# A chunked recurrence on 64x64 quarters of the TensorE array, in six slots a chunk with a fixed order on every engine

## The chip, the cores and the metric

The program runs on one core of a Trainium2 chip. The metric is the time of one execution on the device, in microseconds (us). The profile is one execution, recorded by the hardware profiler; its rows give starts from the beginning of the span.

## The reference

A trunk of two layers on 1024 tokens of width 1024. Layer 0 is attention (sliding window and dilated) and a gated feed-forward block; layer 1 is an RWKV-7 time mix and a second feed-forward block; a norm ends it. All is float32. The change lies in the time mix, whose core is a recurrence over the tokens with one 64x64 state for each of 16 heads:

```python
def step(state, inp):
    r_t, w_t, k_t, v_t, a_t, b_t = inp
    sa = jnp.einsum('bhvk,bhk->bhv', state, a_t)
    state = state * w_t[:, :, None, :] + sa[..., None] * b_t[:, :, None, :] + v_t[..., None] * k_t[:, :, None, :]
    return state, jnp.einsum('bhvk,bhk->bhv', state, r_t)
```

After it every head's output is normed over its 64 values, scaled (`lnx_w`, `lnx_b`), a bonus `sum(r*k*r_k) * v` is added, the result is multiplied by a gate `g`, and an output projection with `w_o` follows.

## The kernel before

The recurrence is computed in 16 chunks of 64 tokens (`NC`). Inside a chunk it is a set of 64x64 products for each head and one triangular solve; only the 64x64 state `S` goes from chunk to chunk. Heads stand in eight pairs, the even head on partitions 0 to 63 and the odd one on 64 to 127, and the pairs in two groups of four.

`rwkv_dense` (L1038) makes, in two halves of 512 tokens (`q`), what the chunks need, and stores it in DRAM: `ar` (decayed `kk` and `r`), `bm` and `km` (the transposed keys, with the masked products against `r` beside them), `nk`, `n` (the triangle that is to be inverted), `v`, the gate `gT` and the bonus factors `bon`. `solve` (L1071) inverts 32x32 triangles by 31 steps of two VectorE operations (L1085, L1086) and stores them as `u` and `ut`. Four solves are needed; the last, `solve(1, 1, ve)`, is handed on as a function (L1367) and runs within the recurrence, at chunk 1.

`Scan` (L1370) loads. `load` (L1428) brings a chunk's `ar`, `bm`, `km`, `nk`, `vb`, some 2 MB; `load2` (L1396) brings, for a pair of chunks, `u` and two small operands `ub` and `nb`. Each has two buffers, so loads run one chunk ahead. `inverse` (L1409) joins the 32x32 inverses of a pair of chunks to 64x64 ones: eight products `nb`, `ub`, four copies, eight products, four copies; `u`'s upper corner is copied first (L1419).

`rwkv_scan` (L1442) is the recurrence. In `step` (L1477), for each of the two groups:

- `o1`: `nk` times `vb`, plus `ar` times `S` (L1486 to L1492); the lower half feeds the solve, the upper half is part of the output.
- `rb`: the lower half, copied by ScalarE and VectorE (L1494, L1495) into the two diagonal blocks of a 128x128 tile whose other blocks are zero. `S`, `rb`, `sb`, `nk` and `vb` are all such block diagonals, so that one 128-row product serves two heads.
- `z`: `u` times `rb` (L1498), copied to `sb` in two halves (L1499, L1500).
- `o2`: `km` times `vb` plus `bm` times `sb` (L1502, L1504).
- The new state: for each head of the pairs VectorE adds `o2` and `S` (L1512), GpSimd multiplies by the decay `el` (L1513).
- The output `y`: the upper halves of `o1` and `o2` (L1519, L1520).

`finish` (L1524), once for two chunks: mean, centring, square, variance, the power -1/2 on GpSimd (L183), scaling by it and by `lw`, the bonus (`vn`, the values again, loaded by `load3` and multiplied by `bo`, L1538), eight transposes on TensorE, the gate (L1549) and the split into two float32r parts (`t.split`, L154) for the output projection.

The program is written with a scheduler that orders instructions on each engine by a simulated timeline; `chained` fixes the order within one accumulation alone. The recurrence's first instructions are thus placed among the dense stage's last. DMAs all go through SyncE's (SP's) queue, one after another; one that waits for a buffer holds back those behind it. PSUM is given out as p1, pz, p2 with two banks each and pq, pg with one.

Of the kernel before, what the change touches and what calls it, by code (L numbers as in the profile page):

```python
# [21 lines left out]
P = 128  # L22
T = 1024
# [1014 lines left out]
def rwkv_dense(t, hp, sv, hT, first):  # L1038
# [11 lines left out]
    d["bon"] = dp.tile([T, 16], F32, name="bon_d")  # L1050
# [20 lines left out]
    def solve(q, g, eng):  # L1071
# [9 lines left out]
        po.memset(u.rearrange("p i j -> p (i j)")[:, 0:1024:33], 1.0)  # L1081
        for s in range(31):
            i, j = s + 1, 31 - s
            w3 = sv.tile([P, 256], F32, name="sw", tag="sw")[:, :i * j].rearrange("p (i j) -> p i j", j=j)
            eng.tensor_tensor(w3, u[:, :i, s:s + 1].broadcast_to([P, i, j]), n[:, s:s + 1, s + 1:].broadcast_to([P, i, j]), MUL)  # L1085
            eng.tensor_tensor(u[:, :i, s + 1:], u[:, :i, s + 1:], w3, ADD)  # L1086
        ac.copy(n[0:64], u[0:64].rearrange("p i j -> p j i"))
# [7 lines left out]

        return store
# [15 lines left out]
    for q in range(2):  # L1112
# [251 lines left out]
        ve.tensor_copy(bs, transposed(bon)[:, :, 0:16])  # L1364
        nc.sync.dma_start(d["bon"][ts].rearrange("(b p) h -> p b h", p=P), bs)
    es.close()
    return d, scan, lambda: solve(1, 1, ve)  # L1367


class Scan:  # L1370


    def __init__(self, t, d):
# [4 lines left out]
        self.nb, self.ub, self.tb, self.u2 = (self.zeroed(lp, n, 1, 8, 64)[0] for n in ("nb", "ub", "tb", "u2"))  # L1378
        self.zs = [(self.zeroed(lp, "nk0", 1, 2, 5, 64)[0], self.zeroed(lp, "vb0", 1, 2, 8, 64)[0])]
        self.pools, self.us, self.tiles = [lp], [None, None], [None, None]  # L1380

    def zeroed(self, pool, name, n, *shape):
        r = [pool.tile([P, *shape], F32, name=f"{name}{i}") for i in range(n)]
        for x in r:
            self.t.nc.gpsimd.memset(x, 0.0)
        return r
# [5 lines left out]
    def more(self, sp):  # L1392
        self.pools.append(sp)
        self.zs.append((self.zeroed(sp, "nk1", 1, 2, 5, 64)[0], self.zeroed(sp, "vb1", 1, 2, 8, 64)[0]))

    def load2(self, g):  # L1396
        nc, d, half = self.t.nc, self.d, self.half
        u = self.pools[g % 2].tile([P, 8, 2, 64], F32, name="u", tag="u")
        q, i = divmod(2 * g, 8)
        nc.sync.dma_start(u, d["u"][q, :, :, i:i + 2])  # L1400
        self.us[g % 2] = [u[:, :, cc] for cc in range(2)]
# [7 lines left out]
    def inverse(self, g, pq):  # L1409

        pe, ac = self.t.nc.tensor, self.t.nc.scalar
        us = self.us[g % 2]
        ps = pq.tile([64, 8, 64], F32, name="pq", tag="pq")
# [26 lines left out]


def rwkv_scan(t, d, ld, sv, last):  # L1442

# [194 lines left out]
```

## Time and profile before

| what | us |
|---|---|
| three runs | 2832.75, 2835.06, 2835.6; median 2835.06 |
| the profiled execution | 2844.29 |
| its span | 2842.5 |
| first product with a state (chunk 1) | 1861.94 |
| first product of the output projection after the recurrence | 2072.56 |

The mean granted TensorE clock of the profiled execution is 0.967. In a row of grouped instructions the line stands first, then engine, operation, the output and the inputs by name (digits left out, so `o1` and `o2` are both `o`), the shapes, the count, and after a bar the busy time in us and the mean duration of one in ns; after the next bar the idle time of the engine before them and what ended it. A float32 matmul of the program stands as two records, each with a weight load (PEld). A matmul's shape is given as rows x columns of the array that it uses, then the moving operand.

### The profile page before, as it was taken

The numbers are of one execution on the slowest core, as the hardware profiler recorded it, in microseconds if no ns is written. First come the engines' busy times: TensorE is split into PE (matmuls) and PEld (weight loads), VectorE is DVE, ScalarE is ACT, GpSimd is POOL, SyncE is SP. The second block draws the span as 40 slices with busy tenths as digits, with TensorE's granted clock in tenths as the row PEclk, the third lists the DMA queues.
The fourth block names the chain that finished last, engine by engine and source line by source line (L and its number), as shares of the span: only waits on it lengthen the run. The fifth ranks groups of instructions, "written<-read, shape, count | busy, mean of one in ns | idle before, by whom it ended". The sixth has DMA issues, their size and how long they took to land. (4 is left out here: it accounts for less than half of the span.)

```text
span 2842.5 us, 38023 instructions
## 1 busy us (share of the span) xinstructions
PE 2660.4 (94%) x13302; PEld 2123.9 (75%) x13302; DVE 1781.8 (63%) x3017; ACT 1203.2 (42%) x2377; POOL 1101.3 (39%) x830
## 2 busy tenths in 40 slices
PE   8999997989999999998998899888998999999998
PEld 6777775678888877775676667777877888887776
DVE  4554564566434448789658888767666544344987
ACT  3445445334333333345644454434334433333434
POOL 1221221335343416445443533335643544331644
PEclk9999999999999999999999899789999999999999
DMA  4111112632222246452465276788753222225654
GB/s 139 45 38 53 38 53 80 209 106 89 80 84 85 74 159 226 148 177 89 157 165 161 82 219 162 202 210 211 209 174 104 98 81 83 81 71 196 212 156 159
DMA packets 301536, 367.18 MB, mean 129 GB/s; under 512 B 101000, under 2 KB 175112, under 8 KB 301344
## 3 DMA queue, kind: packets, MB, share of 16 engines
q1 hardware_dynamic: 296560, 351.08, 40.2%
q10 hardware_dynamic: 4496, 12.62, 1.1%
q8 instruction: 105, 1.72, 0.3%
q0 software_dynamic: 288, 1.05, 0.1%
q14 instruction: 87, 0.71, 0.1%
HBM read 268.98 MB, written 95.68 MB: 128 GB/s over the span
## 5 line engine op out<-in xcount | busy, mean ns | idle before, releaser
L919 PE MATMUL pd<-ws,as 128*128 128x512 f32 x1848 | 431.8, 395 | 24.0 <-DVE ws L154 23.0
L919 PEld LDWEIGHTS pd<-ws,as 128*128 128x128 f32 x1848 | 350.1, 190 | 103.7 <-DVE ws L154 28.6
L771 PE MATMUL y<-t,cw 128*128 128x512 f32 x1584 | 370.2, 389 | 0.0
L771 PEld LDWEIGHTS y<-t,cw 128*128 128x128 f32 x1584 | 297.3, 188 | 62.4
L154 DVE TENSOR_TENSOR cw<-raw,cw 128x512 fp32r<-128x512 f32 x264 | 216.4, 822 | 199.6 <-ACT cw L154 196.0
L154 ACT CAST cw<-raw 128x512 fp32r<-128x512 f32 x264 | 163.2, 621 | 245.8 <-PE z L771 103.3
L154 DVE TENSOR_TENSOR wl<-raw,wh 128x512 fp32r<-128x512 f32 (+1 forms) x146 | 146.0, 1002 | 105.4 <-ACT wh L154 105.3
L154 ACT CAST wh<-raw 128x512 fp32r<-128x512 f32 (+1 forms) x154 | 119.9, 779 | 205.8 <-PE mm L174 53.6
L780 POOL TENSOR_TENSOR c<-c 128x512 f32<-128x512 f32 x66 | 111.7, 1692 | 186.5 <-DVE c L787 135.3
L173 PE MATMUL mm<-hx,wh 128*128 128x512 f32 x384 | 163.8, 427 | 0.0
L775 ACT COPY sn<-y 128x512 f32<-128x512 f32 x132 | 76.9, 587 | 196.4 <-PE y L771 193.1
L175 PE MATMUL mm<-hx,wl 128*128 128x512 f32 x384 | 152.3, 397 | 0.0
L174 PE MATMUL mm<-hx,wh 128*128 128x512 f32 x384 | 151.6, 395 | 0.0
L771 PE MATMUL z<-b,cw 128*128 128x512 f32 x576 | 142.5, 398 | 6.6 <-DVE tx L717 6.6
L257 POOL TENSOR_TENSOR ry<-ry,S 128x512 f32<-128x512 f32 x40 | 51.8, 1294 | 217.2 <-DVE ry L256 192.7
L771 PEld LDWEIGHTS z<-b,cw 128*128 128x128 f32 x576 | 110.9, 193 | 31.0 <-issue 7.0
L154 ACT CAST as<-raw 128x512 fp32r<-128x512 f32 x110 | 68.2, 620 | 154.0 <-PE pd L919 81.5
L771 PE MATMUL y<-b,cw 128*128 128x512 f32 x528 | 129.0, 394 | 0.0
L771 PE MATMUL z<-t,cw 128*128 128x512 f32 x528 | 123.3, 389 | 0.0
L813 POOL TENSOR_TENSOR raw<-s,raw 128x512 f32<-128x512 f32 x44 | 59.6, 1355 | 151.8 <-DVE cw L154 151.6
L787 DVE TENSOR_TENSOR c<-z,sn 128x512 f32<-128x512 f32 x92 | 63.4, 689 | 84.8 <-ACT sn L775 74.4
L771 PE MATMUL x<-b,cw 128*128 128x512 f32 x480 | 116.1, 396 | 0.0
(469 smaller groups left out, 6129.6 us busy)
## 6 DMA issues: line engine op xcount, KB each, us to landing
raw<-act SPq DMA_DIRECT2D x132, 256.0 KB, 3.4
raw<-in_wd SPq DMA_DIRECT2D x132, 256.0 KB, 3.1
raw<-in_wg SPq DMA_DIRECT2D x88, 256.0 KB, 2.9
raw<-in_wu SPq DMA_DIRECT2D x88, 256.0 KB, 2.6
act<-c SPq DMA_DIRECT2D x88, 256.0 KB, 2.0
raw<-in_wrk SPq DMA_DIRECT2D x32, 512.0 KB, 4.4
raw<-in_win SPq DMA_DIRECT2D x24, 512.0 KB, 3.5
raw<-in_wout SPq DMA_DIRECT2D x32, 256.0 KB, 3.5
```

Source lines behind the costliest of these rows:

```text
L154: return self.nc.scalar.copy(hi, src), (eng or self.nc.vector).tensor_tensor(lo, src, hi.bitcast(F32), SUB)
L173: seen(mm(ps, lh, rh, start=start, stop=False))
L174: seen(mm(ps, lh, rl, start=False, stop=False))
L175: seen(mm(ps, ll, rh, start=False, stop=stop))
L257: nc.gpsimd.tensor_tensor(y, y, self.S[:, s], MUL)
L771: seen(pe.matmul(ps, w[:, x, s], bs[:, k, y], start=start and k == j == 0, stop=k == 3 and j == 2, skip_group_check=True))
L775: ac.copy(s, ps)
L780: po.tensor_tensor(g, g, u, MUL)
L787: ve.tensor_tensor(c[-1], z, s, ADD)
L813: po.tensor_tensor(a11, s, a11, SUB)
L919: pe(ps[b], s[:, x, t], w[:, y], start=first and i == 0, stop=f == N - 1 and i == 2, skip_group_check=True)
```

## The change

Six things change, all in the recurrence.

1. **Quarters.** No tile is a block diagonal any more. Every matmul is 64x64x64, of one head, in one quarter of the array: rows by the operands' partitions (`r`), columns by the output's (`r` or `o`, the other half). Loops go over `both`, so that the half alternates from one matmul to the next; where `to` (the new state) and `y` (the output) are made, their matmuls alternate too. The state is added to `to` by a product with an identity `eye`, and the output's `ar` part goes straight into `y`'s bank.
2. **Copies.** `rb` is one ScalarE copy of 128x256, `sb` one VectorE copy, the new state one VectorE product with the decay, `y` one ScalarE copy. GpSimd has no part in the state.
3. **Slots and order.** A chunk has six slots. Each of the two groups is a generator of three stages a chunk (up to the `rb` copy, up to the `sb` copy, up to `y`); group 0 goes in slots 0, 2 and 4, group 1 in slots 3, 5 and 1 of the next chunk. `own` chains every compute instruction of the recurrence to the one before on its engine, in written order. DMAs are not chained.
4. **Inverse, centring and finish** are cut into pieces and put in given slots. The bonus is no longer made of `vn`: `diag` makes diagonal 64x64 blocks of `bo`, and `turned` computes `v` times that block and adds the transposed `y` by products with `eye`, so that the bonus comes with the transposes.
5. **The last solve** is a generator, `solving`; it takes one step in slot 0 (its loads) and two steps a slot from slot 8 on. Its stores follow the last step.
6. **Loads** run two chunks ahead, in three buffers (`vb` in eight, since `turned` reads it later); the order of a chunk's loads is `ar`, `nk`, `vb`, `km`, `bm`. `u` keeps two buffers; `load2` of the next pair stands in slot 11 of a pair, after the middle stage of group 1 in the odd chunk. `bon` is stored with even and odd heads apart; zeroed tiles other than the inverse's four fall away.

The core of the diff:

```diff
+            xz = p1.tile([P, 2, 4, 64], F32, name="xz", tag="xz")
+            for i, e, r, o in both:
+                mm(xz[r, 0, i], nk[r, k0 + i], vb[r, k0 + i], start=i == 0, stop=c == 0)
+            if c:
+                for i, e, r, o in both:
+                    mm(xz[r, 0, i], ar[r, k0 + i, 0:64], S[r, i], start=False, stop=True)
+            rb, sb = (tp.tile([P, 4, 64], F32, name=n, tag=f"{n}{g}", bufs=1) for n in ("rb", "sb"))
+            own(ac.copy(rb, xz[:, 0]))
+            yield
+            to, y = (p2.tile([P, 4, 64], F32, name=n, tag=n) for n in ("to", "yo"))
+            if c:
+                for i, e, r, o in both:
+                    mm(to[r, i], eye[r], S[r, i], start=i == 0, stop=False)
+                    mm(y[o, i], ar[r, k0 + i, 64:], S[r, i], start=i == 0, stop=False)
+            for i, e, r, o in both:
+                mm(to[r, i], km[r, k0 + i, 0:64], vb[r, k0 + i], start=c == i == 0, stop=False)
+                mm(y[o, i], km[r, k0 + i, 64:], vb[r, k0 + i], start=c == i == 0, stop=False)
+            for i, e, r, o in both:
+                mm(xz[r, 1, i], u[r, k0 + i], rb[r, i], start=True, stop=True)
+            own(ve.tensor_copy(sb, xz[:, 1]))
+            yield
+            for i, e, r, o in both:
+                mm(to[r, i], bm[r, k0 + i, 0:64], sb[r, i], start=False, stop=True)
+                mm(y[o, i], bm[r, k0 + i, 64:], sb[r, i], start=False, stop=True)
+            if c + 1 < NC:
+                S = Ss[c % 2]
+                own(ve.tensor_tensor(S, to, d["el"][:, k0:k0 + 4, c:c + 1].broadcast_to([P, 4, 64]), MUL))
...
+            own(ac.copy(ys[c // 2][:, c % 2, k0:k0 + 4], y))
+            yield
```

The inverse of pair `g` from slot `s` on, `finish`, and the loop over the slots:

```diff
+        at(s + 1, product, ld.nb, ld.ub)
+        at(s + 7, product, ld.tb, ld.u2)
+        for i, x in enumerate(quarters):
+            at(s + i, take, "u2", *x)
+            at(s + 2 + i, take, "tb", *x)
+            at(s + 8 + i, take, "us", *x)
+        at(s + 11, lambda: g + 1 < NB and ld.load2(g + 1))
...
+            for cc in range(2):
+                for i, e, r, o in both:
+                    out, k = got[j][r, i, cc * 64:cc * 64 + 64], 4 * j + i
+                    if which == 0:
+                        mm(out, vbs[cc][r, k], dg[r, cc, k], start=i == cc == 0, stop=False)
                     else:
+                        mm(out, y[o, cc, k], eye[o], start=False, stop=True)
...
+        at(s + 4, diag)
+        at(s + 7, rstd)
+        at(s + 10, scale)
+        at(s + 12, affine)
+        for j in range(2):
+            at(s + 11 + 6 * j, turned, j, 0)
+            at(s + 15 + 6 * j, turned, j, 1)
+            at(s + 15 + 6 * j, gated, j)
+            at(s + 17 + 6 * j, rest, j)
...
+    for c in range(NC + 1):
+        for j in range(6):
+            slot = 6 * c + j
...
+                if (j % 2 == 0 or j in (3, 5) and c < NC) or (j == 1 and c):
+                    next(groups[j % 2])
+            if c < NC and j == 1 and c + 2 < NC:
+                ld.load(c + 2)
+            if j == 0 and c % 2 == 0 and c + 2 < NC:
+                inverse(c // 2 + 1, slot)
+            if j == 1 and c:
+                centre(c - 1, slot)
+                if c % 2 == 0:
+                    finish(c // 2 - 1, slot)
+            if solved and (slot == 0 or slot >= 8):
+                for _ in range(2 if slot else 1):
+                    store = next(solved, None) if solved else None
...
+            run(slot)
```

More of the change, by code (lines that the diff above doesn't have):

```diff
@@ L1069, in rwkv_dense, with solving @@
     mg = t.cst[:, CMG:CMG + P]
[L1071 removed]
+    def solving(q, g, eng, own=lambda x: x):
         n, u = (sv.tile([P, 32, 32], F32, name=n, tag=n) for n in ("n", "ub"))
@@ L1377, in __init__ @@
         lp = self.lp.pool
[L1378 to L1386, printed above, removed]
+        self.nb, self.ub, self.tb, self.u2 = (lp.tile([P, 8, 64], F32, name=n) for n in ("nb", "ub", "tb", "u2"))
+        for x in (self.nb, self.ub, self.tb, self.u2):
+            t.nc.gpsimd.memset(x, 0.0)
+        self.sp, self.us, self.tiles = None, {}, {}
     def begin(self):
@@ new lines, in rwkv_scan, with own, mm @@
+    p1, p2, pq, pg = (pool(n, b, space=PSUM) for n, b in (("sp1", 2), ("sp2", 2), ("spq", 1), ("spg", 1)))
+    ld.sp = sp
+    half = ld.half
+    before = {}
+    def own(ins):
+        eng = str(ins.ins.engine)
+        if eng in before:
+            t.after(ins, before[eng])
+        before[eng] = ins
+    def mm(*x, **k):
+        own(pe.matmul(*x, **k, skip_group_check=True))
+    eye = sp.tile([P, 64], F32, name="eye")
+    for r in half:
+        po.tensor_copy(eye[r], t.ident[r, r])
+    both = [(i, e, half[e], half[1 - e]) for i in range(4) for e in range(2)]
@@ new lines, in inverse, with product, take @@
+    def inverse(g, s):
+        us, got = ld.us[g], []
+        quarters = [(cc, e) for cc in range(2) for e in range(2)]
+        def product(x, y):
+            got.append(pq.tile([64, 8, 64], F32, name="pq", tag="pq"))
+            for k in range(8):
+                mm(got[-1][:, k], x[:, k], y[:, k], start=True, stop=True)
+        def take(f, cc, e):
+            o = cc * 64 + e * 32
+            own(ac.copy(*{"u2": lambda: (ld.u2[o:o + 32, :, cc * 32:cc * 32 + 32], us[cc][e * 64 + 32:e * 64 + 64, :, 32:64]),
+                          "tb": lambda: (ld.tb[o:o + 32, :, e * 32:e * 32 + 32], got[0][e * 32:e * 32 + 32, :, cc * 32:cc * 32 + 32]),
+                          "us": lambda: (us[cc][e * 64:e * 64 + 32, :, 32:64], got[1][e * 32:e * 32 + 32, :, cc * 32:cc * 32 + 32])}[f]()))
+        at(s + 1, product, ld.nb, ld.ub)
[5 more added lines that the diff above has]
+        at(s + 11, lambda: g + 1 < NB and ld.load2(g + 1))
@@ new lines, in run @@
+    def run(slot):
+        for f, x in slots.pop(slot, ()):
+            f(*x)
+    inverse(0, -12)
+    for s in range(-12, 0):
+        run(s)
+    ld.load(1)
+    lw = sp.tile([P, 8, 64], F32, name="lw")
+    bo = sp.tile([P, NC, 8], F32, name="bo")
+    for e in range(2):
+        nc.sync.dma_start(lw[half[1 - e]], a["lnw"].rearrange("o (k e v) -> o e k v", e=2, v=64)[:, e].broadcast_to([64, 8, 64]))
+        nc.sync.dma_start(bo[half[e]], d["bon"][:, e].rearrange("(c t) k -> t c k", t=64))
@@ L1586, in rwkv_scan @@
+    for slot in range(6 * NC + 6, 6 * NC + 30):
+        run(slot)
+    assert not slots
     es.close()
```

252 lines of the change are left out of this document (94 added, 158 removed).

## The prediction

> **What bounds the kernel now.** I read the page first, then the stages around the recurrence, then the groups of instructions in it, and last who waits for whom.
>
> ```profile
> span 2842.5 us, 38023 instructions
> PE 2660.4 (94%) x13302; PEld 2123.9 (75%) x13302; DVE 1781.8 (63%) x3017; ACT 1203.2 (42%) x2377; POOL 1101.3 (39%) x830
> ```
>
> TensorE carries the whole span. The change touches only the recurrence, so its own stage counts. Two rows of the timeline bound it: the first product with a state (chunk 1), and the first product of the output projection that follows.
>
> ```profile
> 1861.94 1.16 PE L1492 MATMUL o<-S,ar 128*128 128x128 f32 x8
> ...
> 2072.56 0.19 PEld L173 LDWEIGHTS po<-wh,o 128*128 128x128 f32 x1
> ```
>
> That is 210.6 us for chunks 1 to 15, 14.0 us each (chunk 0 runs among the last dense products). The stages, in columns span, PE, PEld, DVE, ACT, POOL, clock, DMA share, GB/s:
>
> ```profile
> 1845.00:1862.00 17.00, 16.56 (x85) 13.67 (x83) 5.54 (x18) 4.74 (x10) 1.11 (x2) 0.65 0.68 132
> ...
> 1862.00:1943.00 81.00, 64.83 (x496) 56.94 (x496) 67.65 (x134) 26.86 (x59) 35.68 (x30) 0.94 0.78 210
> 1943.00:2066.00 123.00, 109.92 (x882) 96.18 (x880) 83.16 (x166) 52.89 (x119) 72.52 (x59) 0.97 0.78 214
> ```
>
> VectorE leads in the first 81 us (84% busy: it also solves the last group of triangles there); later TensorE does (89%), and DMA is near three quarters all along. The waits say why none is full:
>
> ```profile
> ACT rb L1494 <- PE o L1492: 52.7, 20, 6.4
> POOL S L1513 <- DVE se L1512: 44.5, 18, 8.6
> ...
> SPq L1433 <- PE o L1504: 16.3, 6, 5.8
> SPq L1433 <- PE o L1502: 16.3, 8, 3.1
> ```
>
> The first two are the loop of the recurrence (TensorE, copy, TensorE, copy, sum, product); the last two are loads one chunk ahead, which wait in SP's order until the chunk before gives its buffer up.
>
> **TensorE under the change.** A float32 matmul stands as two records. Now a chunk has 80 records on the whole array or half its columns, 8 a chunk for transposes, 16 for the inverse: 104. Under the change I count, for each of two groups: 8 matmuls with `nk`, 8 with `ar`, 16 with `eye` and `ar`, 16 with `km`, 8 with `u`, 16 with `bm`: 72, so 144 a chunk; `turned` adds 64 in two chunks and `inverse` 16 in two chunks. That is 184 matmuls, 368 records, 3.5 times as many, each 64x64x64. All depends on how many run side by side. Rows of the whole span, equal shapes set beside each other:
>
> ```profile
> L1498 PE MATMUL z<-rb,u 128*64 128x128 f32 x256 | 36.0, 287 | 9.3 <-DVE rb L1495 8.6 <-ACT tm L1348 0.3
> L490 PE MATMUL pv<-pT,vtA 128*64 128x128 f32 x360 | 26.5, 281 | 2.0 <-ACT pT L483 1.6
> L1334 PE MATMUL pg<-ar,bk 64*128 64x128 f32 x512 | 77.4, 308 | 7.6 <-DVE bk L1322 5.9 <-DVE tm L1338 1.7
> L454 PE MATMUL sc<-kT,q 64*128 64x128 f32 x104 | 9.7, 298 | 0.0
> L1101 PE MATMUL bon<-r,cst 128*32 128x128 f32 x128 | 7.7, 319 | 1.5 <-DVE r L1323 1.5
> ```
>
> L1498 always writes one column half: 36.0/256 = 141 ns a record. L490 alternates column halves: 74 ns. L1334 stays in one row half: 151 ns; L454 alternates row halves: 93 ns. L1101 goes round four column groups: 60 ns. So neighbours on different parts of the array run together, two nearly for the price of one. The new loops alternate `e`, hence diagonal quarters, and in the `to`/`y` loops all four. No row shows quarters of both kinds at once; I take full overlap, since rows and columns each show it. The price of one round with 64 moving columns is from an inverse:
>
> ```profile
> 2004.35 1.01 PEld L1423 LDWEIGHTS pq<-u,tb 128*64 128x64 f32 x16 [0.91 <-ACT u L1419]
> ```
>
> 1.01/16 = 63 ns. Rounds a chunk: `nk`, `ar`, `u` 8 each (two at a time), the three `to`/`y` loops 8 each (four at a time): 48 a group, 96 a chunk, 6.0 us. `inverse` has no neighbours: 16 records, 1.0 us. `turned` goes two at a time: 32 rounds, 2.0 us. Together 9.1 us. Changing between array forms costs
>
> ```profile
> PEld o L1486 <- issue: 4.8, 19, 1.7
> ```
>
> 0.25 us each; now there are about eight changes a chunk, then only those around two products in two chunks: 4 x 0.25 / 2 = 0.5 us. TensorE then needs 9.6 us a chunk.
>
> **The loop of the recurrence.** The copies fall from two engines in turn to one each of 128x256:
>
> ```profile
> L1494 ACT COPY rb<-o 64x256 f32<-64x256 f32 x30 | 11.0, 365 | 53.0 <-PE o L1492 52.7
> L1500 DVE COPY sb<-z 64x256 f32<-64x256 f32 x30 | 12.5, 418 | 14.2 <-ACT sb L1499 13.7
> L1513 POOL TENSOR_TENSOR S<-se,el 64x256 f32<-64x256 f32 x56 | 37.0, 661 | 46.6 <-DVE se L1512 44.5
> ```
>
> The width along a partition is the same, so 0.37 and 0.42 us; the two L1513 steps of 0.66 us leave the loop, as the state is added by `eye` on TensorE. Each copy is covered by the other group's slot: `rb` has a slot of `bm` and 16 rounds before its reader (1.5 us), `S` a whole middle stage (1.5 us), `sb` only the other group's first stage, 16 rounds = 1.0 us against 0.42 us and two hand-overs. All fit if the copying engine is free; if not, `sb` is late first.
>
> **VectorE.** In a chunk: four operations of 0.42 us, two reductions of half the width, and in two chunks eight gate products and two remainders:
>
> ```profile
> L1534 DVE TENSOR_REDUCE var<-sqy 128x16 f32<-128x1024 f32 x7 | 8.5, 1211 | 1.4 <-ACT sqy L1533 1.3
> L1549 DVE SCALAR_TENSOR_TENSOR yg<-pg,vec,gt 128x128 f32<-128x128 f32 x48 | 13.5, 344 | 3.5 <-PE pg L1546 3.2
> L154 DVE TENSOR_TENSOR o<-yg,o 128x512 fp32r<-128x512 f32 x12 | 12.4, 1042 | 2.1 <-ACT o L154 1.8
> ```
>
> 1.7 + 1.2 + 0.2 + 8 x 13.5/48 / 2 (1.1) + 1.0 = 5.2 us, off the path. But the solve sits at two steps a slot from slot 8 to 24, in VectorE's fixed order ahead of the next slot's copies:
>
> ```profile
> 1862.00:1945.00 83.00, 16.41 (x31) 0.94 0.78 209
> ...
> 1862.00:1945.00 83.00, 17.44 (x31) 0.94 0.78 209
> ```
>
> These are the two lines of the solve (L1085, L1086; columns span, VectorE, clock, DMA share, GB/s), 33.9 us, some of it slowed by its neighbours. With 2.7 chunks x 3.1 us (no `finish` gates yet) that is 42 us of VectorE in 16 slots; I take 40 us (below, without the slowing, 34).
>
> **Loads.** Here the bytes of the scan's window and its queue's share:
>
> ```profile
> DMA packets 52193, 43.34 MB, mean 205 GB/s; under 512 B 24144, under 2 KB 43215, under 8 KB 52175
> ...
> q1 hardware_dynamic: 52175, 43.10, 75.2%
> ...
> vn<-v_d SPq DMA_DIRECT2D x8, 512.0 KB, 4.9
> ...
> nb<-n_d SPq DMA_DIRECT2D x23, 32.0 KB, 3.8
> ```
>
> 43.1 MB at a share of 0.752 in 211 us is 272 GB/s when full. The change drops `vn` (8 x 0.52 = 4.2 MB), moves the rest: 38.9 MB, 143 us, 9.5 us a chunk. So DMA stands level with TensorE, and being two chunks ahead removes the two SP waits above, not this floor. One load cannot run ahead: `u` has two buffers, so the next pair's `u` starts when the odd chunk's last `u` product ends, and ScalarE's fixed order waits for it in the next slot. The nearest row is ScalarE's wait for it now:
>
> ```profile
> ACT u L1419 <- DMA u<-u_d: 7.7, 5, 2.1
> ```
>
> 7.7 us in five loads, 1.5 us each, 0.8 us a chunk. Behind it stand the next `y` and `rb` copies, and TensorE's middle stage waits for `rb`; most of that is under its other products, so I put 0.5 us a chunk, between nothing and the 2.8 of the first rival.
>
> **What costs nothing.** ScalarE has four copies of 0.37 us, a half-width square, and in two chunks twelve pieces of the inverse and two casts:
>
> ```profile
> L1419 ACT COPY u<-u 32x256 f32<-32x256 f32 x24 | 9.7, 402 | 7.9 <-DMA u<-u_d 7.7
> L183 POOL TENSOR_TENSOR rs_r<-rs_v,mhalf 128x16 f32<-128x16 f32 x7 | 20.4, 2908 | 13.2 <-DVE rs_v L181 7.7 <-PE o L1488 5.4
> L1540 POOL TENSOR_TENSOR y<-y,lw 128x1024 f32<-128x1024 f32 x7 | 16.5, 2357 | 0.5
> q8 instruction: 105, 1.72, 0.3%
> ```
>
> With the pieces at 0.4 us that is about 5 us a chunk. GpSimd's half-width centring and, in two chunks, three products near 2.4 us and the power of 2.9 us make 6 us. Both lie under 10 us of products; uncovered, they would add themselves. The instruction queue brought 1.72 MB; 3.5 times the scan's share of TensorE's instructions adds about 0.5 MB. `lw`, `bo`, the reordered `bs` and the dropped memsets are a few short steps among dense work.
>
> **Sum.** TensorE 9.6 + 0.5, with DMA 9.5 beside it and some of each not overlapping: 10.6 us a chunk. Chunk 1 to slot 8 and the 12 chunks after the solve: 12.3 x 10.6 = 131 us; solve stretch 40 us; 3 us for the fixed order starting among the dense tail. 174 against 210.6: 37 us less. The tail (`finish` of the last pair) lay under the output projection and still does. The profiled run took 2844.3 us around its 2842.5 us span, so 2807 there; the median of the three timed runs is 2835.1, so **2798 us**. Own range: a chunk of 9.6 and a solve stretch of 34 us (152 us, 2777) to a chunk of 11.8 and 45 us (190 us, 2815).
>
> **Rivals.**
>
> *Late inputs of the inverse.* Issues on SP take this long (nb; u as least, median, most in ns, first and last start):
>
> ```profile
> 1875.41 0.59 SPq L1407 DMA_DIRECT2D nb<-n_d  x1
> L1400 SPq DMA_DIRECT2D u<-u_d x6: 552/558/609, 1876.8 to 2023.5; - x6
> ```
>
> If SP issues `ub` and `nb` behind the waiting `u`, six issues of 0.6 us follow and the last lands 3.8 us later: 0.6 + 3.6 + 3.8 = 8.0 us, less the 2.5 us of products in between (`nk` and `ar`, `turned`, `bm`: 16 + 16 + 8 rounds). TensorE, in fixed order, stands 5.5 us in two chunks: 10.6 + 2.8 = 13.4 us a chunk, 12.3 x 13.4 + 43 = 208 us, 2832. For it: the written order. Against: at 1875.4 `nb` goes ahead of `u`.
>
> *The clock (slower).* From 1845 to 1862 TensorE was busy 16.56 of 17.0 us, yet the clock stood at 0.65. A burst there, on row halves, ran at 236 ns a record against 151 on average:
>
> ```profile
> 1847.94 3.78 PE L1334 MATMUL pg<-ar,bk 64*128 64x128 f32 x16
> ```
>
> If matmuls on part of the array do not keep the clock up, 10.1 us become 15.5 us: 15 x 15.5 + 3 = 236 us, 2860. It turns into a loss below a clock of 0.72 (10.1/14.0). Against: L490 and L454 alternate halves at the rates above. The Trainium skill, TensorE: Matmul & The Clock Gate, Part 1, has the clock follow how busy TensorE has recently been; by that rule the denser stage keeps full clock, and the sum above stands, but the 0.65 row speaks against busy time alone as the measure.
>
> *Same bank (slower).* If two row halves cannot write one PSUM bank together, the diagonal loops run singly: 48 + 32 more rounds of 63 ns, 5.0 us, 15.6 us a chunk, 237 us, 2861. No run here has that pattern: L454 writes a tile per row half, L490 one tile from both column halves. The Trainium skill, TensorEngine Tiling (Array Packing), Restrictions and Gotchas, states that different row tiles cannot use one bank at the same time, which speaks against this change; the diagonal quarters, though, write disjoint partitions, as L490's halves do.
>
> *No overlap at all,* the change not doing what it says: 368 x 63 ns = 23.2 us a chunk, 355 us, 2980. Break-even is 38 ns a record.
>
> *Better than the sum:* rounds in bursts longer than sixteen cost less than 63 ns and DMA without `vn` runs over its present pace, 9.0 us a chunk, and 34 us: 145 us, 2769 or less.
>
> **How the numbers follow.** A measurement tells about 0.2% (6 us) here. Forecast 0.56, better 0.07, late inputs 0.16 (half of it faster, the rest even), clock 0.12, bank 0.06, no overlap 0.03. Faster 0.71, same 0.08, slower 0.21. The range 2768 to 2850 takes in the forecast, the late inputs, and most of the better case; of the slower ones only mild forms.
>
> **What would show it.** Right: from the first `ar` product to the output projection 174 us, chunks near 10.6 us after slot 24 and 15 us between slots 8 and 24, 368 records a chunk at 25 to 30 ns, clock over 0.9, DMA share over 0.85, no SP wait for the chunk before. Wrong: records over 38 ns apart, a clock near 0.65, TensorE or ScalarE waiting for `ub`, `nb` or `u` over 5 us in two chunks, or `sb` waiting behind VectorE in every slot.

## The result, and the profile after

The changed kernel takes 2860.28 us (median of four runs, 2855.49 to 2862.39); beside it the kernel before took 2834.05. The ratio is 1.009, with a 95% interval of 1.0073 to 1.0107: slower by 26 us. The forecast was 2798, faster, with a range of 2768 to 2850. The profiled execution took 2859.83 us around its span; that of the kernel before took 2844.29, 9 us over its median, so the two profiles differ by 15.5 us and not by 26:

```profile
span 2857.8 us, 46158 instructions
```

The two rows that bound the recurrence, as in the prediction: the first product with a state (group 0 of chunk 1) and the first product of the output projection.

```profile
1860.82 0.84 PE L1457 MATMUL xz<-S,ar 64*64 64x64 f32 x13
...
2074.68 0.79 PE L173 MATMUL po<-wh,o 128*128 128x512 f32 x1
```

213.9 us, where it had been 210.6 and 174 was forecast. The output projection then runs from 2074.68 to the start of its last product at 2182.4, 107.7 us; before, from 2072.56 to 2167.4, 94.8 us. So 3 us were lost in the recurrence, and 13 behind it, where the prediction had put nothing. The stages of the kernel after, over the same stretches as those of before (span, PE, PEld, DVE, ACT, POOL, clock, DMA share, GB/s):

```profile
1845.00:1862.00 17.00, 11.72 (x237) 10.78 (x236) 3.26 (x8) 6.67 (x18) 1.11 (x2) 0.62 0.90 176
1862.00:1943.00 81.00, 49.02 (x1722) 45.98 (x1712) 45.14 (x111) 24.33 (x58) 23.37 (x13) 0.83 0.73 201
1943.00:2066.00 123.00, 91.08 (x3431) 87.08 (x3431) 48.56 (x116) 42.86 (x105) 50.01 (x27) 0.92 0.57 167
```

No engine is full any more: TensorE is busy 61% and 74% where it was 80% and 89%, VectorE 56% and 39%, and the DMA share falls to 0.57 in the long stretch. The clock is lower. Who waits for whom, from 1862 to 2070 (total, times, longest):

```profile
ACT u L1520 <- DMA u<-u_d: 37.6, 5, 8.8
...
PE to L1457 <- DVE sb L1495: 17.9, 6, 13.3
DVE wl L154 <- ACT wh L154: 15.3, 1, 15.3
ACT wh L154 <- DMA raw<-in_wo: 14.7, 1, 14.7
...
PE xz L1457 <- issue: 12.8, 8, 3.7
PE to L1457 <- issue: 11.8, 8, 4.0
...
PE yo L1457 <- issue: 9.8, 7, 2.5
...
PE pg L1457 <- issue: 4.9, 5, 1.6
```

The last four rows are the news: TensorE stands still 28 times, 39.3 us in all, for nothing that the profile shows. In the kernel before such waits made 4.4 us. They lie in the middle of loops:

```profile
1998.41 0.22 PE L1457 MATMUL yo<-vb,km 64*64 64x64 f32 x1
...
1998.83 0.22 PE L1457 MATMUL yo<-vb,km 64*64 64x64 f32 x1
2002.80 0.48 PE L1457 MATMUL xz<-rb,u 64*64 64x64 f32 x4 [3.75 <-issue]
```

Counted in the trace, the records between two such gaps are 125 to 128 almost every time, or two, three or six times that. A record goes with a weight load, so 128 records are 256 instructions; the instruction queue brings its bytes in packets of 16,384, 64 bytes for each of 256. So I read these waits as TensorE's instructions being fetched, with TensorE faster than the fetch. The packets of that queue (count, MB, share of 16 engines), from 1943 to 2066, in the kernel before and in the kernel after, and then in the whole of the kernel after:

```profile
q8 instruction: 7, 0.11, 0.4%
```

```profile
q8 instruction: 28, 0.46, 1.6%
```

```profile
q8 instruction: 138, 2.26, 0.3%
```

Set on one clock, packets and gaps look like this (kernel after, worked out from the trace: four pieces in a row; us from the first record of a piece):

```
first record   piece run   next fetch starts   takes   landed to next record   next piece after
2046.71        3.26        +1.85               1.09    1.33                    4.27
2050.99        2.78        +1.17               1.33    1.42                    3.91
2054.90        2.77        +1.06               1.18    1.39                    3.64
2058.53        2.95        +1.26               1.29    1.39                    3.94
```

A piece runs in about 3 us, but the fetch of the next never starts sooner than 1.05 us after this one has begun, takes 0.9 to 1.7, and 1.2 to 1.7 us after it has landed the first matmul starts. So a piece costs 3.5 us at best. These four lie where hardly any loads run; over all 21 pieces that lie between two such gaps the start has a median of 1.4 us and goes to 5.8, and the next piece comes after 3.5 to 8.1 us. The time from landing to the first matmul hardly moves (1.2 to 1.7 us), however late the fetch, which fits a TensorE that goes on when its packet is there.

How much they weigh is plainest in chunks 4 to 15, where little else is late. First chunks 1 to 3, then these twelve, up to the last `bm` product:

```profile
1860.82:1909.19 48.37, 26.89 (x918) 25.06 (x915) 30.00 (x78) 11.41 (x30) 6.43 (x4) 0.75 0.71 199
1909.19:2070.48 161.29, 118.23 (x4432) 112.67 (x4432) 67.01 (x156) 57.26 (x136) 71.35 (x40) 0.93 0.60 173
```

The twelve chunks take 13.4 us each. TensorE is busy for 9.9 of these and waits 3.3 for nothing (39.0 of the 39.3 us lie here) and 0.3 for all else.

### The profile page after: what moved, and what is told of

Same layout as the page of the kernel before. It is cut to its first block, busy times and chain, and to the rows that moved or that the text cites. A ratio compares the mean times of both kernels' runs of the same rounds, so it can differ in the third digit from the quotient of the medians.

```text
span 2857.8 us, 46158 instructions
## 1 busy us (share of the span) xinstructions
PE 2634.8 (92%) x17510; PEld 2112.7 (74%) x17510; DVE 1715.2 (60%) x2939; ACT 1187.9 (42%) x2359; POOL 1055.9 (37%) x772
## 3 DMA queue, kind: packets, MB, share of 16 engines
q1 hardware_dynamic: 294288, 346.62, 39.3%
q8 instruction: 138, 2.26, 0.3%
q0 software_dynamic: 288, 1.05, 0.1%
## 4 chain that ended last, share of the span: by engine, by line
PE 54%; DVE 15%; DMA 6%; issue 4%; ACT 2%; POOL 2%; SPq 1%; DVEq 0%; POOLq 0%; ACTq 0%
PE y L771 17%; PE z L771 9%; PE pd L919 7%; PE x L771 3%; DVE ws L154 2%; DMA raw<-in_wd 2%; PE po L173 2%; PE pg L1344 2%; PE po L174 2%; PE po L175 2%; PE pz L173 1%; PE xz L1457 1%; DVE as L154 1%; PE pz L174 1%; PE pz L175 1%
## 5 line engine op out<-in xcount | busy, mean ns | idle before, releaser
L771 PEld LDWEIGHTS y<-t,cw 128*128 128x128 f32 x1584 | 297.3, 188 | 62.4
L154 DVE TENSOR_TENSOR cw<-raw,cw 128x512 fp32r<-128x512 f32 x264 | 215.4, 818 | 198.5 <-ACT cw L154 192.5
L771 PEld LDWEIGHTS y<-b,cw 128*128 128x128 f32 x528 | 98.8, 187 | 22.7
L154 DVE TENSOR_TENSOR as<-raw,as 128x512 fp32r<-128x512 f32 x110 | 97.6, 888 | 29.5 <-ACT as L154 29.3
```

The lines of the kernel that those rows point to most:

```text
L154: return self.nc.scalar.copy(hi, src), (eng or self.nc.vector).tensor_tensor(lo, src, hi.bitcast(F32), SUB)
L771: seen(pe.matmul(ps, w[:, x, s], bs[:, k, y], start=start and k == j == 0, stop=k == 3 and j == 2, skip_group_check=True))
```

## The experiments

Two theories stood at first: that single late inputs stop a loop whose order is fixed (the first 25 us, then `u`), and that TensorE's array and the loads set a chunk. Fetch came as the third, out of the first four traces. Every edit makes the program's scheduler place the dense stage anew: the first product with a state falls between 1842.5 and 1862.4, and that is in each median. So I judge mechanisms by the stretch from there to the output projection, and give the median beside it. All from the profiled executions, but for median and ratio; "issue" is the sum of TensorE's waits for nothing, "half clock" the time at a granted clock of 0.50 within the stretch. A stretch is read from one execution, and whole runs of one kernel lie 4 to 18 us apart, so a few us in a stretch decide nothing by themselves:

| kernel | first product | stretch | issue | half clock | projection | median | ratio to before |
|---|---|---|---|---|---|---|---|
| before | 1861.9 | 210.6 | 4.4 | 17.1 | 94.8 | 2834.05 | |
| after | 1860.8 | 213.9 | 39.3 | 50.0 | 107.7 | 2860.28 | 1.0073 to 1.0107 |
| e1_wo_held | 1848.7 | 215.6 | 35.7 | 62.4 | 107.0 | 2853.96 | 1.0045 to 1.0097 |
| e2_u_three | 1854.5 | 208.0 | 36.0 | 44.1 | 108.3 | 2859.96 | 1.0055 to 1.0111 |
| e3_solve_out | 1852.8 | 207.6 | 37.1 | 40.5 | 109.2 | 2851.13 | 1.0042 to 1.0082 |
| e4_both | 1851.9 | 209.8 | 39.1 | 42.8 | 106.4 | 2848.15 | 1.0041 to 1.0075 |
| e5_fewer | 1862.4 | 215.1 | 3.6 | 45.8 | 106.5 | 2858.52 | 1.0068 to 1.0104 |
| e6_narrow | 1855.4 | 212.9 | 36.4 | 53.0 | 107.0 | 2858.49 | 1.0069 to 1.0109 |
| e7_more | 1854.2 | 235.3 | 43.7 | 71.4 | 106.9 | 2871.35 | 1.0112 to 1.0150 |
| e8_joined | 1853.4 | 207.1 | 4.0 | 40.4 | 108.1 | 2855.47 | 1.0057 to 1.0096 |
| e9_state | 1854.3 | 204.9 | 29.9 | 44.5 | 107.6 | 2844.06 | 1.0037 to 1.0062 |
| e10_half_loads | 1857.9 | 198.5 | 28.1 | 38.5 | 106.8 | 2839.54 | 1.0015 to 1.0038 |
| e11_x_first | 1855.8 | 210.0 | 35.2 | 43.0 | 114.9 | 2859.09 | 1.0085 to 1.0113 |
| e12_best | 1856.4 | 226.0 | 14.3 | 68.3 | 104.0 | 2858.43 | 1.0076 to 1.0107 |
| e13_queue | 1847.4 | 208.1 | 37.8 | 47.3 | 107.1 | 2851.23 | 1.0042 to 1.0078 |
| e14_tail | 1853.0 | 212.1 | 36.0 | 55.1 | 96.7 | 2843.16 | 1.0021 to 1.0047 |
| e15_queue_state | 1852.5 | 202.1 | 26.4 | 48.4 | 107.0 | 2837.34 | 1.0005 to 1.0030 |
| e16_queue_state_u | 1847.2 | 224.7 | 31.6 | 53.0 | 97.6 | 2852.65 | 1.0045 to 1.0087 |
| e17_depth_two | 1842.5 | 215.3 | 36.8 | 46.2 | 106.2 | 2848.54 | 1.0038 to 1.0071 |
| e18_no_order | 1847.1 | 250.3 | 20.3 | 85.3 | 105.4 | 2879.72 | 1.0143 to 1.0173 |

### Late inputs: e1 to e4

**e1_wo_held**: the first casts of the output projection's weights are ordered behind slot 84.

```diff
         self.splits = self.split(hi[:p], lo[:p], raw[:p], eng)
+        for ins, earlier in zip(self.splits, self.held):
+            self.after(ins, earlier)
...
+            if slot == 84:
+                t.held = tuple(ran[n] for n in ("ac", "ve"))
```

> Kernel after with one order added: the casts that split the output projection's first weights (ScalarE wh, VectorE wl) come behind the recurrence's slot 84 on their engines. Theory A (VectorE's order): the two long stalls of TensorE ahead of bm products, 5.3 us at 1852 and 13.3 us at 1866, are sb copies standing behind a wl step that waits for a weight load far back in SP's queue. Then both go, the last bm product comes 15 to 19 us earlier than 2070, and the time is 2842 to 2846 instead of 2860. Theory B (the loads in SP's queue are late as such): sb or its inputs stall on something else at the same place, and under 5 us is gained, 2856 or more. Neither changes chunks 4 to 15.

The stall that it is about, in the kernel after: VectorE's rows, and then TensorE's.

```profile
1862.27 0.42 DVE L1502 TENSOR_TENSOR S<-to,el 128x256 f32<-128x256 f32 x1 [1.54 <-PE to L1457]
1878.00 0.69 DVE L154 TENSOR_TENSOR wl<-raw,wh 128x512 fp32r<-128x512 f32 x1 [15.31 <-ACT wh L154]
1878.61 0.42 DVE L1495 COPY sb<-xz 128x256 f32<-128x256 f32 x1
```

```profile
1879.08 0.37 PE L1457 MATMUL to<-sb,bm 64*64 64x64 f32 x1 [13.32 <-DVE sb L1495]
```

TensorE had nothing left to do at 1866, and `sb` would have been next; but VectorE's order has a weight split of the next stage ahead of it, whose load SP issued only at 1871 and ScalarE's cast waited for:

```profile
1871.48 1.18 SPq L167 DMA_DIRECT2D raw<-in_wo  x1
1877.35 0.62 ACT L154 CAST wh<-raw 128x512 fp32r<-128x512 f32 x1 [14.67 <-DMA raw<-in_wo]
```

With the order added that wait is gone, and another stands there: `S` behind the solve's first step, which waits 9.0 us for its `n` (in e4_both 10.2):

```profile
DVE sw L1093 <- DMA n<-n_d: 9.0, 1, 9.0
```

The stretch is no shorter (215.6), so theory A was right on the place and wrong on the gain: behind one late input there was the next.

**e2_u_three**: `u` gets a third buffer, `load2` comes in slot 3 instead of 11.

> Kernel after with a third buffer for u and load2 of the next pair issued eight slots earlier. Theory A (ScalarE's wait for u sets the even chunks): ScalarE's 37.6 us of waits for u in five loads fall under 5 us, even chunks go from 14.5 us to 11.5 or 12 as the odd ones, and 7 pairs at 2.5 us make 15 to 18 us: 2843 to 2846. Theory B (the inverse's sixteen lone products and its ScalarE pieces set the even chunks): the wait goes, but the even chunks stay within 1 us, and the time stays within 6 us of 2860.

ScalarE's waits for `u` did not go (30.2 us in four), so the run does not show what their end would bring. The stretch lost 6 us, the median nothing. Theory A's expectation failed.

**e3_solve_out**: the last solve does one of its 31 steps; the rest is left out.

> Kernel after without 30 of the 31 steps of the last solve (part of the computation left out). Theory A (my prediction's: the solve holds VectorE between slots 8 and 24 and with it the loop): chunks 1 to 4 fall to 10.6 us from 24, 15, 12 and 14, about 20 us less, 2840. Theory B (the stall there is the weight split in VectorE's order): the 13.3 us stall stays, chunks 2 and 3 lose 2 or 3 us together, 2855 to 2860.

The stretch is 6 us shorter; chunk 1, from group 0's first product with a state to that of chunk 2, still takes 21.1 us (22.1 in the kernel after) and TensorE's wait for `sb` is still there, 12.8 us. The solve was not what held the loop: theory B.

**e4_both**: the edits of e1 and e2.

> The order of e1_wo_held and the third buffer of e2_u_three together. If both are causes and independent, 30 to 36 us less than 2860, 2824 to 2830, faster than before by 0.2 to 0.4%. If only the first is, 2842 to 2846. If the products' price is the limit (chunks at 12 us without any stall), no chunk after the solve falls under 12 us. If my chunk of 10.6 us is right where nothing stalls, odd and even chunks come to 10.6 to 11.5.

Stretch 209.8, median 2848.15: neither sum came. Chunks 4 to 13 take 11.3 to 16.1 us with both edits (ScalarE still waits 27.2 us for `u`), and the gaps named "issue" make 39.1 us. That turned me to them.

### Fetch: e5 to e7, e9, e10

**e6_narrow**: 32 of 64 moving columns in the `km` and `bm` products (half of state and output left out), for example

```diff
-                mm(to[r, i], bm[r, k0 + i, 0:64], sb[r, i], start=False, stop=True)
+                mm(to[r, i, w], bm[r, k0 + i, 0:64], sb[r, i, w], start=False, stop=True)
```

> Kernel after with 32 instead of 64 moving columns in all products with km and bm after chunk 0 (half of the new state and of the output left out); as many instructions, 32 of the 96 rounds a chunk at about half the length. Theory F: a piece still takes 4.3 us, chunks stay at 12 to 14 us, 2856 to 2862. Theory A (array time): 32 x 0.03 = 1 us a chunk, 15 us less, 2845.

2858.49, stretch 212.9: the time stayed. But this does not rule theory A out, since the rounds did not get shorter. The first and the last of 32 records with `km`, in the kernel after and in e6_narrow:

```profile
1998.40 0.22 PE L1457 MATMUL to<-vb,km 64*64 64x64 f32 x1
1998.83 0.22 PE L1457 MATMUL yo<-vb,km 64*64 64x64 f32 x1
```

```profile
1993.51 0.19 PE L1457 MATMUL to<-vb,km 64*64 64x32 f32 x1
1993.91 0.22 PE L1457 MATMUL yo<-vb,km 64*64 64x32 f32 x1
```

That is 13.8 ns a record with 64 moving columns and 12.9 with 32, and TensorE's busy time in the stretch did not fall (149.5 us, 147.0 in the kernel after). The expectation "about half the length" was wrong, and the run leaves the question open.

**e7_more**: 32 products of one zero column are added in each chunk.

```diff
+            for i, e, r, o in both:
+                mm(to[r, i, 0:1], eye[r], none[r], start=False, stop=False)
+                mm(y[o, i, 0:1], eye[r], none[r], start=False, stop=False)
```

> Kernel after with 32 added products a chunk of one moving column that is zero: 64 records more a chunk, half a piece of 16 KB, and hardly any time on the array. Theory F: half a piece, 2.1 us a chunk, 30 us more, 2885 to 2895, and as many pieces on the instruction queue. Theory A: 16 short rounds a chunk at 30 ns or less, 0.5 us, 2862 to 2868.

The stretch grew by 21.4 us, 1.4 a chunk, with 50 packets in it instead of 43; the median grew by 11. That lies between the two theories' numbers and does not choose between them: 32 of the added records, of one moving column, start within 0.40 us, 12.9 ns apart, so they were not short on TensorE either.

```profile
1988.47 0.17 PE L1457 MATMUL to<-none,eye 64*64 64x1 f32 x1
1988.87 0.19 PE L1457 MATMUL yo<-none,eye 64*64 64x1 f32 x1
```

TensorE's busy time in the stretch grew by 24 us (147.0 to 170.8; half clock 71.4 us instead of 50.0), its waits for fetch by 4.4.

**e9_state**: no products with `eye`; VectorE adds the state.

```diff
-                    mm(to[r, i], eye[r], S[r, i], start=i == 0, stop=False)
...
+                    own(ve.tensor_tensor(sm, to, S, ADD))
```

> Kernel after without the products with eye; the old state is added by VectorE before the decay. 336 matmul records a chunk instead of 368; the loop with ar loses every second record, and 16 records at 30 ns two at a time take what 32 at 15 ns four at a time took, so the array's time is the same. Theory F (a piece of 128 records costs some 4.3 us of fetch): 2.63 pieces instead of 2.88, 1.1 us a chunk, 13 to 16 us less, 2844 to 2848. Theory A (array time and waits for loads): no gain, up to 5 us more for VectorE's added step in the loop.

2844.06, as theory F had it; 9 us of the 16 are in the stretch (39 packets instead of 43, 2.3 us each), the rest ahead of it. The waits for fetch fell by those 9 us (39.3 to 29.9), TensorE's busy time by 3.5. Against theory A, a step more in the loop and hardly less time on the array made it faster. Of the runs on fetch this is the one that separates the two theories.

**e5_fewer**: `km` and `bm` products of state and output become one of 64x128, and the copies two halves.

```diff
-                mm(to[r, i], bm[r, k0 + i, 0:64], sb[r, i], start=False, stop=True)
-                mm(y[o, i], bm[r, k0 + i, 64:], sb[r, i], start=False, stop=True)
+                mm(ty[e][:, i], bm[r, k0 + i], sb[r, i], start=False, stop=True)
```

> Kernel after, with the two quarter products of each head with km (state and output) made one 64x128x64 product, and those with bm likewise; 304 matmul records a chunk instead of 368, the same number of rounds on the array, and two half copies in place of one for the state and for y. Theory F (fetch: TensorE's instructions come in pieces of 16 KB, one for 128 matmul records with their weight loads, and a piece takes 4.3 us at least): 2.4 pieces a chunk instead of 2.9, 10.3 us instead of 12.4, some 30 us less, 2828 to 2838. Theory A (the array's time, 63 ns a round, and waits for loads): no gain, or up to 6 us slower by the added copies, 2858 to 2866.

The waits for fetch went (3.6 us), the time did not (2858.52). The expectation "the same number of rounds" was wrong: in these rows of e5_fewer two row halves that write all 128 columns start together every 0.11 us, where four quarters of the kernel after took 0.06 (32 records from 1998.40 to 1998.83).

```profile
1996.25 0.27 PE L1457 MATMUL to<-sb,bm 64*128 64x64 f32 x1
1996.26 0.27 PE L1457 MATMUL yo<-sb,bm 64*128 64x64 f32 x1
1996.37 0.27 PE L1457 MATMUL to<-sb,bm 64*128 64x64 f32 x1
1996.37 0.27 PE L1457 MATMUL yo<-sb,bm 64*128 64x64 f32 x1
```

From 1985 to 2060 TensorE is now full with fewer records; the first row is e5_fewer's, the second that of the kernel after:

```profile
1985.00:2060.00 75.00, 71.10 (x1814) 66.49 (x1816) 35.87 (x88) 32.60 (x82) 35.03 (x20) 0.98 0.58 181
```

```profile
1985.00:2060.00 75.00, 55.40 (x2119) 52.95 (x2113) 31.32 (x73) 25.55 (x62) 34.05 (x18) 0.93 0.55 163
```

At 55 ns a record a piece of 128 lasts 7 us, longer than its fetch takes, and the waits are gone. Fewer instructions help only if the array does not pay for them.

**e10_half_loads**: `km` and `bm` are loaded for three chunks only (the rest left out).

> Kernel after without the loads of km and bm from chunk 3 on (their products run on the first three chunks' data; half of the bytes of a chunk are left out). Theory D: a fetched piece costs 3.7 us when the DMA queues are quiet (as in the last chunks) and more only because its packet starts behind the loads; then every fetch starts 1.1 to 1.4 us after the piece before begins, chunks of 2.9 pieces take 10.7 us instead of 13.2, and 25 us go, 2830 to 2836. If a fetch has a latency of its own, apart from the loads: cycles of 4 to 6 us stay and the time stays over 2852.

15 us less in the stretch, 21 in the median; waits for fetch 28.1 instead of 39.3. So waits for fetch depend on the loads. But theory D had every fetch start after 1.1 to 1.4 us, and that failed: in the pieces between two gaps the median is 1.4 us, as in the kernel after, and single ones still go to 3.9 (5.8 there). How a load delays a fetch is not shown.

### The passage, the tail, and sums: e8, e11 to e16

**e11_x_first**: in the projection, from row 4 on, a weight load comes behind the load of `x_d`.

> Kernel after with one order on SP: in the output projection the weight load of rows k (from the fifth on) comes behind the load of the residual x that is written just ahead of it. Theory T1 (in the tail a wait for x_d of 4.5 us and the half clock after it are the larger part of the 13 us): the output projection takes 100 us instead of 107.7, 2851 to 2854. Theory T2 (the eight blocks of 32 records of the last pairs' transposes, 7 us of TensorE, are): 2857 to 2861. The scan is as in kernel after.

The projection took 114.9 us, so theory T1's expectation failed. But the run does not price the wait for `x_d`: it went, and two waits for weights, 7.5 us together, came in its place.

**e14_tail**: the eight blocks of `turned` of the last two pairs are left out but for four matmuls.

> Kernel after with the transposes and bonus products of the last two pairs (eight blocks of 32 records) left out but for one matmul in each of four places. Theory T2 (these blocks are what the tail lost, six of them among the output projection): the projection takes 101 us instead of 107.7, 2852 to 2855. Theory T3 (the tail's loss is the wait for x_d and the half clock that follows): no more than 2 us.

The projection takes 96.7 us, 11.0 less, and the kernel 2843.16, 17 us less, of which 7.8 are the earlier start; more than T2 gave. Those blocks are what the tail lost: six of them, 1.15 us each, stand among TensorE's products there, and the stall with the half clock behind it went with them. In the kernel after it reads so, first the wait, then the windows around it:

```profile
2111.71 0.79 PE L173 MATMUL po<-wh,o 128*128 128x512 f32 x1 [4.49 <-DVE x L688]
```

```profile
2096.00:2110.60 14.60, 11.22 (x130) 8.77 (x128) 5.71 (x13) 3.27 (x6) 0.00 (x0) 1.00 0.44 136
2110.60:2117.40 6.80, 5.69 (x13) 4.45 (x14) 3.44 (x5) 1.18 (x3) 0.00 (x0) 0.50 1.05 401
```

**e13_queue**: e1, and GpSimd issues the loads of `n`, `bo` and `lw`.

> e1_wo_held, and the loads of the last solve's triangles (n) and of bo and lw issued by GpSimd instead of SP. Theory S (at the passage from the dense stage SP issues some 50 DMAs one behind another between 1840 and 1880, and what the fixed orders of VectorE and ScalarE wait for, first the weights, then n, is late in it): chunk 1 falls from 24 or 20 us to 14 or less, the last bm product comes 15 to 20 us ahead of kernel after's 2070, 2842 to 2848. Rival: another input from SP's queue (nb, km, nk) takes the place of n, chunks 1 and 2 still have a stall of 8 us or more, 2852 to 2856.

The last `bm` product comes at 2051 instead of 2070; but 13 of those 19 us are the earlier start. Chunk 1 takes 16.9 us; `n` is no longer among the waits, three smaller ones of 3 to 4 us are. 2851.23: partly theory S.

**e15_queue_state**: e13 and e9.

> e13_queue and e9_state together. If the early stalls and the fetch are separate causes, their gains add: 14 to 18 us and 16 us, 2826 to 2832, level with the kernel before or a little faster. If the stall only moves, 2838 to 2844.

2837.34: e9's 16 us and e13's 9 add nearly, 23 together. It is the best of the runs that leave nothing out, and still 0.05 to 0.30% slower than before.

**e16_queue_state_u**: e15 with the third `u` buffer and earlier loads from pair 2 on.

> e15_queue_state with a third buffer for u and an earlier load2 from pair 2 on. If ScalarE's waits for u (27 to 31 us in four pairs) hold the loop once fetch is cheaper, even chunks after chunk 3 lose 1 to 2 us each and 6 to 10 us go against e15_queue_state; if they lie beside the fetch, the two are equal within 3 us.

The last `bm` product came 5.6 us sooner (2043.8 against 2049.4), and 5.3 of these are the earlier start, so this third buffer brought nothing (ScalarE still waits 26.6 us for `u`). Then the projection began 28 us later, because the scheduler put the last pairs' blocks, with the waits between them, ahead of its first product:

```profile
2057.75 1.98 PE L1462 MATMUL pg<-eye,y 64*64 64x64 f32 x32 [4.45 <-POOL y L1566]
2061.10 1.97 PE L1462 MATMUL pg<-dg,vb 64*64 64x64 f32 x32 [1.38 <-DVE yg L1587]
2063.38 1.97 PE L1462 MATMUL pg<-eye,y 64*64 64x64 f32 x32 [0.30 <-ACT fence L1582]
```

It then took 97.6 us, as in e14 without these blocks: they were moved, not hidden, and the median is 15 us above e15's.

**e8_joined** (e4, e5, and the solve from slot 12) and **e12_best** (e4, e9, e11, the solve from slot 12, and `nk` in block diagonals, `mm(xz[:, 0, i], nk[:, k0 + i], vb[:, k0 + i], ...)`):

> e4_both and e5_fewer together, and the last solve's steps from slot 12 instead of 8. If fetch sets a chunk and the two early stalls and the u wait come on top: chunk 1 under 15 us, the rest 10.3 to 11.5, last bm product 30 to 45 us ahead of kernel after's, 2810 to 2825, faster than before by 0.3 to 0.9%. If the array sets it, as e4_both, 2846 to 2850.

> e4_both, e9_state and e11_x_first together, the last solve's steps from slot 12, and the products with nk as four of the whole array (nk in block diagonals, vb stacked): 320 records a chunk, 2.5 pieces, at the same array time. Theory F: 10 to 11.5 us a chunk, the scan 150 to 165 us instead of 210, the output projection 100 us: 2805 to 2822, faster than before. If chunks stay at 13 us, 2835 to 2842.

Both missed. e8 has the array's price of e5. In e12 waits for fetch fell to 14.3 us, but TensorE was busy 163 us up to the last `bm` product instead of 145, a wait of 9.4 us for `nb` took the place of `n`, and the projection began 26 us after the last `bm` product, as in e16.

### Two parts undone: e17, e18

**e17_depth_two** (`DEEP = 2`) and **e18_no_order** (`own` does nothing):

> Kernel after with two buffers instead of three for a chunk's loads, so that they run one chunk ahead (the sixth part of the change undone). Prediction's theory (SP's waits for the chunk before cost the kernel before up to 2 us a chunk and go with the third buffer): 10 to 20 us slower than kernel after, 2870 to 2880. Theory F (a chunk of 12 to 13 us is set by fetch, and the next chunk's loads fit beside it): within 5 us of 2860.

> Kernel after without the chains that fix the order on each engine (the scheduler places the recurrence by its simulated timeline). If the written order is what turns one late input into a stall of the whole loop: the early stall of 13 us and the u waits shrink, 2840 to 2852. If the order is what lets the two groups cover each other: 2865 or more. Theory F alone: as many pieces of instructions, chunks of 12 us or more wherever TensorE's records stand close, 2852 to 2865.

Without the third buffer the stretch is the same (215.3) and the median 12 us lower, all of it by an earlier start. Without the order the stretch is 250.3: TensorE waits 57.6 us for `sb` in 22 places. The order is worth 36 us in it; it also lets one late input stop everything.

## Why the prediction was wrong, point by point

**TensorE's products: right.** "I take full overlap": 32 records of four quarters in 0.43 us, 14 ns each, and diagonal pairs at 28 to 30 ns, as in this row of the kernel after (0.67 us is the sum of 15 starts and one matmul of 0.22).

```profile
1993.48 0.67 PE L1457 MATMUL xz<-vb,nk 64*64 64x64 f32 x16
```

So "same bank" and "no overlap" are out; diagonal quarters write one bank side by side, where records without a neighbour (the inverse's) start 58 ns apart. The page of the Trainium skill cited there (TensorEngine Tiling, Restrictions and Gotchas) states that different row tiles cannot use one bank at the same time; here they do, and the measurement decides. TensorE was busy 140 us in the two long windows, 9.6 us a chunk over 14.6 chunks, half-clock time included. That this is the forecast's 9.6 is in part luck: at full clock a round took 55 to 58 ns where 63 had been put, and the half clock made up for it.

**The step that failed** stood under what costs nothing: "The instruction queue brought 1.72 MB; 3.5 times the scan's share of TensorE's instructions adds about 0.5 MB." It did bring 0.54 MB more (2.26), and I gave that no time. It is the change's main cost: 39.3 us of waits, where the fetch had been put at nothing. Chunks 4 to 15 were to take 12 x 10.6 = 127 us and took 161.3, 34 more; the waits for fetch in them are 39.0. I had looked at bytes and share of the queue (0.3%), not at how long one packet takes against how long 128 records run. The Trainium skill, Runtime: NRT & Kernel Launch, Instruction fetch mechanics, has instructions come in 16 KiB blocks of 256 by a DMA queue, and calls the crossing of a block mostly hidden. On the blocks the trace agrees; hidden they are in the kernel before (4.4 us of waits), and not at 15 to 30 ns a record.

**"TensorE needs 9.6 us a chunk ... with DMA 9.5 beside it".** Neither was the bound: in chunks 4 to 15 TensorE was busy 118.2 of 161.3 us, with a DMA share of 0.60. The loads count through the fetch (e10).

**The clock.** I gave it 0.12 as a rival, for work on part of the array. It fell from 0.94 to 0.83 and from 0.97 to 0.92, but by gaps: near waits of 1.7 to 13 us the granted clock stands at 0.50 for one to four steps of 3.4 us, 50.0 us of the stretch. That costs at most half of it, 25 us, and less where TensorE was idle anyway. In this stretch each step before a fall had TensorE busy for 19 to 43% of its 3.4 us; at full clock steps with 44% or more were followed by full clock. So waits for fetch of some 1 us do not bring it down: from 2008 to 2073, with none over 2.6 us, it is 1.00. The Trainium skill, TensorE: Matmul & The Clock Gate, Part 1, has a clock of half or full and a window of 3.4 us; on both the trace agrees. Its table has the half clock come after at least one idle window; here it came after windows that were in part busy, and the measurement decides. What brings the clock back is not shown: the kernel before stood at 0.50 from 1836.3 to 1856.8 with TensorE busy all the time. That this rival's sum gave 2860 and that of "same bank" 2861, the measured time, is coincidence: they had some 15.5 us of products a chunk, and the products took 9.9.

**The solve stretch, 40 us.** By e3 the solve costs some 6 us of the stretch, where I had put 11 (40 less 2.7 x 10.6). Chunks 1 to 3 took 48.4 us where 43.5 was forecast (3.5 up to slot 8, then 40): near, but by luck, since most of the excess was another wait. What I had not looked for was the next stage's weight split in VectorE's order: "All fit if the copying engine is free; if not, `sb` is late first" was right, but I had only the solve in mind. 13.3 us, once.

**Loads.** Being two chunks ahead "removes the two SP waits above": they stay, and move.

```profile
SPq L1423 <- PE xz L1457: 23.1, 10, 5.6
...
SPq L1422 <- PE yo L1457: 13.1, 6, 3.5
```

Two chunks ahead bring nothing in the stretch (e17).

**"So I put 0.5 us a chunk", for `u`.** ScalarE waited 37.6 us, 2.5 a chunk. TensorE's waits other than issue are 25 us, of which `sb` and `S` are 21.6 and `u` itself 3.4 (once), so little of it is seen to reach TensorE; no run took the `u` waits away, and their price stays open. The rival's `ub` and `nb` are not among TensorE's waits in the kernel after.

**"The tail (`finish` of the last pair) lay under the output projection and still does."** It cost 13 us, of which e14 shows 11. The new `finish` has four blocks of 32 records a pair on TensorE, six of the last two pairs' eight fall within the projection, and that is the stage that TensorE fills; work is hidden only by a stage that leaves its engine idle.

**Sum.** From the first product with a state to the last `bm` product are 209.7 us. TensorE's waits in it are 64.3 (39.3 issue, 25 others), so it was busy for 145, or 15 x 9.7: what I gave it, 15 x 9.6 = 144, though now with half-clock time in it. For all else the 174 had left 30; it took 64, and 4 more up to the projection. That is 40 us. The tail adds 13. The last 9 are the forecast's step from a profiled execution to the median: before, the profiled one lay 9 us above, and after it does not (2859.83 and 2860.28). 40 + 13 + 9 = 62, the miss.

Open stay what the stretch would be without fetch waits at the same price on the array (no run took all of them away and changed nothing else), the price of the half clock by itself, the reason why some fetches start 3 to 6 us after a piece begins, how the loads delay a fetch, what the `u` waits cost, and why the wait for `x_d` went with e14's blocks (some 4 of its 11 us).

## What to carry to other kernels

When a change cuts matmuls small, count instructions as a resource: a piece of 256 came every 3.5 us at best here, so by an estimate of 3.5 / 128 a run of matmul records, each with its weight load, under some 27 ns a record is limited by the fetch, however well the array overlaps. Before an ablation is read, look in its trace whether it changed what it was to change: half of the columns took nothing off TensorE here. Before fixing an order on an engine, look for what the scheduler will still put into it from the neighbouring stages, and for the last loads that this work waits for; undoing one such wait showed the next each time. Work that spills into the next stage is free only on engines that the stage leaves idle.

## What the runs showed of the hardware

- Fetch of TensorE's instructions: packets of 16,384 bytes. In the 21 pieces between two such waits in the kernel after, the packet takes 0.9 to 1.7 us, starts no sooner than 1.05 us after the piece before began, and 1.2 to 1.7 us pass from landing to the first matmul.
- Four 64x64 quarters run side by side at some 14 ns a record, two diagonal ones at 28 to 30, in one PSUM bank too. With 32 moving columns, and with one, four quarters take 12.9 ns a record (e6, e7). Two row halves of 64x128 take 110 ns a pair (e5), twice the round of four quarters (55).
- The granted clock is 0.50 or 1.00, in steps of 3.4 us; in the kernel after it fell after steps in which TensorE was busy 43% or less.
